# Products of constants in a two-layer trunk's gate and attention, w_glu multiplied whole, and GpSimd's preparation behind a marker

## The chip, the core and the metric

The kernel runs on one core of a Trainium2 chip. Its five engines work side by side, each through its own instructions in order: TensorE (PE, matrix products into PSUM; PEld is its loading of weights), VectorE (DVE), ScalarE (ACT), GpSimd (POOL) and SyncE (SP, which issues most transfers). The metric is the time of one execution in microseconds (us).

## The reference

Two layers over 528 rows (16 learned meta tokens and 512 tokens) of width 1024. Cut to what matters, with every array float32:

```python
for l in range(2):
    hn = rms_norm(h, norm_mix_g[l])
    c_q, c_kv, k_r, u = split(hn @ w_in[l])
    attn = mla_mixer(c_q, c_kv, k_r, ...)       # 4 heads, causal softmax of (q_nope.k_nope + q_rope.k_rope)
    y = complex diagonal state space over u     # 32 groups of 16 channels, 64 states, from a_re, a_im, log_dt, b, c, d
    g = gelu(y)
    ssm = g * sigmoid(g @ w_glu[l])             # w_glu is 512 x 512
    h = h + concat(rms_norm(attn), rms_norm(ssm)) @ w_o[l]
    hn = rms_norm(h, norm_ffn_g[l])
    h = h + (silu(hn @ w_gate[l]) * (hn @ w_up[l])) @ w_down[l]     # hidden width 2816
return rms_norm(h, final_norm_g)[:, 16:]
```

## The kernel before

Everything lies transposed in SBUF: 128 features on the partitions, the rows along the columns. The residual is eight tiles `h` of 128 x 528. The last layer's own part works on the 512 tokens alone.

**Products.** `product` (L268) multiplies one tile of weights with the normalised input. A weight tile comes in by DMA as `raw`. Either it is used whole (`FULL` lists the weights of each layer for which that holds): one float32 product for each 128 x 128 block, at L266. Or it is split: ScalarE casts it to `whi` (L254), VectorE or GpSimd subtracts to get the rest `wlo` (L198, the helper of all two-operand steps), the input is split into a high and a low part in the same way, and each block takes three products (high by high, weight's high by input's low, weight's low by input's high) at L278. With 528 columns each is done in two halves of 264. In layer 0 `w_glu` is whole, in layer 1 it is split, and so is its input `gs`.

**FFN.** `ffn` goes through 22 hidden tiles in three phases of 7, 7 and 8. For each hidden tile it does the gate product into `ga` and the up product into `ua` (eight blocks k = 0 to 7 each), then ScalarE and VectorE form `hid`; at the end of a phase eight down tiles `da` follow. The first gate product of a layer comes right behind the attention's output product: its inputs x[0] to x[7] are made one after the other by ScalarE (L311) and VectorE (L312) as the rows of `h` get their last addend. The sums of squares of the norm (`nacc`, L353) and their spreading over the partitions (`nrb`, L372) are pinned into the first up and the second gate product.

**Order.** The code gives no fixed list: generators are stepped in turn, a scheduler puts each engine's instructions in order by what is ready, and `after(...)` pins an instruction behind another one.

**Preparation of layer 1's state space.** While layer 0's FFN runs, `prep` makes layer 1's tables. `prep_small` computes the parameters on VectorE, by many steps on small tiles (`e`, `q`, `eh`, `el`: powers of the eigenvalues). Then come four quarters; each forms tables `tab` from `eh` and `el` (in layer 1's case on GpSimd, then copied by ScalarE at L595), and two sets of matrices: `bc` from `cc`, then `X`, `Xt`, `C`, `Ct` on GpSimd, transposes on TensorE, a tile `K` with `skip` added, and DMAs out to DRAM. A GpSimd step is placed as soon as its inputs are ready.

**Attention.** `scores` (L1064 to L1070) fills one PSUM block `sc` for each block of queries, the softmax follows on VectorE and ScalarE, `values` transposes the probabilities on TensorE into `ptr` (L1104), copies them to `PT` and multiplies with v into `pvo` (L1125). Between these stand the steps of the state-space scan: `va` (L744) and `ya` (L779 and L780; `S` is its carried state, made by GpSimd). At the program's start 14 products of zeros, bf16 and 512 columns wide, run before any data is there (L221).

Of the kernel before, what the change touches and what calls it, by code (L numbers as in the profile page):

```python
# [22 lines left out]
L = SEQ + NM  # L23
# [19 lines left out]
SING = 0  # L43
WHOLE = 1
PINF = (18, 6)
ACTSW = (0,0)
WIN = ([4,5,7,8,9,6,0,1,2,3],[4,5,0,1,2,3,7,8,9,6])
KB = 1
# [33 lines left out]
          gelu="V", amlo="P", split="V", wmix="P", small="V", ropem="V", nsq="VVVVVVVV", hs="V", woa="P", wos="P")  # L82
WC = 1024

FULL = (("in", "uq", "uk", "uv", "glu", "att", "pv"), ())
SW = 528
LOW, HIGH = 6, 6
BACK = 32
# [14 lines left out]
def trunk(ctx: ExitStack, tc: tile.TileContext, A, out, dbg=None):  # L103
# [151 lines left out]
        tt(lo_on, lo[:, :n], raw[:, :n], hi[:, :n].bitcast(F32), ALU.subtract)  # L255
        return hi, lo

    def product(acc, w, off, xs, cols=(0, L), pins={}, skew=False):
        c0, n = cols[0], cols[1] - cols[0]
        parts = 1 if n <= whole[0] else 2  # L260
        hw = n // parts
        n = len(xs)
        if len(w) == 1:
            for k in range(n):
                for a in range(parts):
                    T.matmul(acc[:, a, 0:hw], w[0][:, off + k * 128:off + (k + 1) * 128], xs[k][:, c0 + a * hw:c0 + (a + 1) * hw],  # L266
                             start=k == 0, stop=k == n - 1)
            return  # L268
        hi, lo = w
        terms = [(k, wt, xi) for k in range(n) for wt, xi in ((hi, 0), (hi, 1), (lo, 0))]  # L270
        if skew:

            terms = [(k, wt, xi) for j in range(n + 1) for k, wt, xi in ((j, hi, 0), (j, lo, 0), (j - 1, hi, 1)) if 0 <= k < n]
        for j, (k, wt, xi) in enumerate(terms):
            c = slice(off + k * 128, off + (k + 1) * 128)
            for a in range(parts):
                with after(pins.get(j)):
                    T.matmul(acc[:, a, 0:hw], wt[:, c], xs[k][:, xi, c0 + a * hw:c0 + (a + 1) * hw],  # L278
                             start=j == 0, stop=j == len(terms) - 1)
# [401 lines left out]

    def prep(l, ea, eb):
        yield from prep_small(l)
        for q in range(4):
            yield from prep_quarter(l, q, ea, eb)

    def prep_quarter(l, q, ea, eb):
        yield from prep_tables(l, q, ea, eb)
        for u in range(2):
            yield from prep_mats(l, q * 2 + u, ea, eb)  # L690
# [170 lines left out]
    def layer(l, nin, nout, nxt):  # L861
# [190 lines left out]
        def scores(hd, Ps):  # L1052
            Pw, off = wide("P"), 0
            for i in range(first_q, 5):
                n, w = (16 if i == 0 else 128), ends[i]
                acc = acc2("sc") if i == 4 else acc1("sc", SCB[i]).unsqueeze(1)
                spans = [(0, 0, max(256, w))] if i < 4 else [(0, 0, HALF), (1, HALF, HALF)]
                qs = slice(tt0[i], tt0[i] + 128)
                for a, s0, sn in spans:
                    o, ks = acc[:, a, 0:sn], slice(s0, s0 + sn)  # L1060
                    if "att" in FULL[l]:
                        T.matmul(o, qn[hd][:, qs], kn[hd][:, ks], start=True, stop=False)
                    for j, (qi, ki) in enumerate(((0, 0), (0, 1), (1, 0))) if "att" not in FULL[l] else ():
                        T.matmul(o, qn[hd][:, qi, qs], kn[hd][:, ki, ks], start=j == 0, stop=False)  # L1064
                    T.matmul(o, qr[hd // 2][:, hd % 2, qs], kr[:, 0, ks], start=False, stop=False)

                    T.matmul(o, qr[hd // 2][:, hd % 2, qs], kr[:, 1, ks], start=False, stop=i == 4 and a == 0)
                dg = acc[:, 0, 0:16] if i == 0 else acc[:, 0, w - 128:w] if i < 4 else acc[:, 1, 136:264]
                mw = 16 if i == 0 else 128
                T.matmul(dg, identb, maskb[:, 0:mw], start=False, stop=True)  # L1070
                sv = acc[0:n, 0, 0:w] if i < 4 else acc[0:n, :, 0:HALF]
                Pi = Pw[:, off:off + w]
                off += w
                po = Pi[0:n, 0:w] if i < 4 else halves(Pi)[0:n]
                st3 = np_.tile([128, 4], F32, tag="st", name="st")
                V.tensor_reduce(out=st3[0:n, 1:2], in_=sv, axis=AX.X if i < 4 else AX.XY, op=ALU.max, negate=True)

                f = rq[0:n, i - first_q:i - first_q + 1]
                mul(V, st3[0:n, 1:2], st3[0:n, 1:2], f)
                S.activation(po, sv, AF.Exp, bias=st3[0:n, 1:2], scale=f, accum_out=st3[0:n, 2:3])  # L1080
                V.reciprocal(out=st3[0:n, 3:4], in_=st3[0:n, 2:3])
                if on("pn", i) is S:
                    S.activation(Pi[0:n, 0:w], Pi[0:n, 0:w], AF.Copy, scale=st3[0:n, 3:4])
                else:
                    on("pn", i).tensor_scalar(out=Pi[0:n, 0:w], in0=Pi[0:n, 0:w], scalar1=st3[0:n, 3:4], scalar2=None, op0=ALU.mult)
                Ps[i] = Pi
                yield

        def values(hd, Ps):
# [6 lines left out]
            for j in range(5):  # L1096
                sn, s0 = (16 if j == 0 else 128), tt0[j]
                x = PT[j]
                b0 = base[j]
                pt = acc2("ptr").rearrange("p a b -> p (a b)") if j == 0 and not c0 else acc1("ptr", PTR[j])  # L1100
                for i in range(max(j, first_q), 5):
                    n = 16 if i == 0 else 128
                    c = 512 if i == 0 else (i - max(j, 1)) * 128
                    T.transpose(pt[0:sn, c:c + n], Ps[i][0:n, s0:s0 + sn], ident[0:n, 0:n])  # L1104
                w = (L if not c0 else 512) if j == 0 else 128 * (5 - j)
                if "pv" in FULL[l]:
                    if j % 2:
                        V.tensor_copy(x[0:sn, 0, b0:b0 + w].bitcast(F32), pt[0:sn, 0:w])
                    else:
                        S.copy(x[0:sn, 0, b0:b0 + w].bitcast(F32), pt[0:sn, 0:w])  # L1110
                else:
                    split((x[0:sn, 0, b0:b0 + w], x[0:sn, 1, b0:b0 + w]), pt[0:sn, 0:w])
                yield
# [160 lines left out]
        for ph in FFN_PHASES:  # L1274
            hid = []
            last = t0 + ph == NHT
            for i in range(t0, t0 + ph):
                wg = wload(A["w_gate"][l, i], V if i >= ONP[0] else P)
                ga = acc2("ga")
                product(ga, wg, 0, nf.xs, nat, {PINF[1]: nf.spread} if i == 1 else {})  # L1280
                if i == 0:
                    nf.F()
                wu = wload(A["w_up"][l, i], V if i >= ONP[1] else P)
                ua = acc2("ua")
                product(ua, wu, 0, nf.xs, nat, {PINF[0]: nf.summed} if i == 0 else {})
                nf.R()
                ev_up(i, ga, ua, hid)
                if i >= NXT[1]:

                    with after(latest(S) if i == NXT[1] else None):  # L1290
                        step(nxt, 2, NXT[0])
# [164 lines left out]
```

## Time and profile before

Three runs took 1321.73, 1325.82 and 1332.43 us. The execution that was profiled took 1328.52 us, with a span of 1326.0 us.

| What | Value |
|---|---|
| median of three runs | 1325.82 us |
| profiled execution, its span | 1328.52 us, 1326.0 us |
| TensorE's mean granted clock over the span | 0.977 |
| share of the span busy: PE, DVE, ACT, POOL | 96%, 59%, 32%, 25% |
| PE's share of the chain that ended last | 72% |
| lines with the largest share of that chain | da, ua and ga at L278: 18%, 18% and 17% |

Busy time counts instructions that run, not what they achieve: a product at half clock is busy for twice as long. The granted clock is a share of full speed, 1.00 being 2.4 GHz. A bracket behind a row of a timeline names the idle time ahead of the row and the instruction that ended it.

### The profile page before, as it was taken

How to read it: one execution, taken by the hardware profiler on the slowest of the kernel's cores; microseconds unless marked ns; L12 is line 12 of the kernel's file. 1: busy time of each engine (PE TensorE's matmuls, PEld its weight loads, DVE VectorE, ACT ScalarE, POOL GpSimd, SP SyncE). 2: the span in 40 equal slices, each digit the busy share in tenths (PEclk: the TensorE clock that was granted, in tenths of full speed). 3: DMA queues.
4: the chain of work that ended last, by engine and by line, in shares of the span. 5: the costliest groups of instructions: out<-in, count | busy, mean ns of one | idle time of the engine just before them, and what ended most of it. 6: DMA issues, size and time to landing. Idle time of an engine off the chain costs nothing.

```text
span 1326.0 us, 20502 instructions
## 1 busy us (share of the span) xinstructions
PE 1276.6 (96%) x8242; PEld 1149.1 (87%) x8242; DVE 779.5 (59%) x1467; ACT 427.5 (32%) x693; POOL 328.4 (25%) x311
## 2 busy tenths in 40 slices
PE   9989999989899999999999999999899999999996
PEld 7777887989899999999999999889788788788885
DVE  8875584496964555355554389665854445435545
ACT  4112454243232222132333226553422222222231
POOL 3101233730572333024204355157200000000001
PEclk9989999999989999999999999699999999999998
DMA  6576442222234344334335447022232323233321
GB/s 219 150 193 160 146 138 88 80 80 82 65 119 147 105 118 107 103 104 120 104 104 161 126 129 216 25 64 65 80 96 86 106 95 91 84 110 92 91 88 64
DMA packets 82575, 145.92 MB, mean 110 GB/s; under 512 B 23344, under 2 KB 49456, under 8 KB 82480
## 3 DMA queue, kind: packets, MB, share of 16 engines
q1 hardware_dynamic: 81184, 143.42, 36.7%
q8 instruction: 64, 1.05, 0.3%
q10 hardware_dynamic: 1296, 1.20, 0.3%
q14 instruction: 31, 0.25, 0.1%
HBM read 121.17 MB, written 23.43 MB: 109 GB/s over the span
## 4 chain that ended last, share of the span: by engine, by line
PE 72%; DVE 9%; ACT 2%; POOL 2%; issue 1%; DMA 1%; DVEq 0%; SPq 0%; POOLq 0%; ACTq 0%
PE da L278 18%; PE ua L278 18%; PE ga L278 17%; PE acc L278 10%; DVE h L198 1%; DVE sq L198 1%; PE acc L266 1%; PE nrb L372 1%; PE pvo L1125 1%; PE pvo L1122 1%; PE nacc L353 1%; DVE wo L198 1%; DVE wlo L198 1%; PE pk L660 1%; POOL tab L198 1%
## 5 line engine op out<-in xcount | busy, mean ns | idle before, releaser
L254 ACT CAST whi<-raw 128x1024 fp32r<-128x1024 f32 (+3 forms) x174 | 174.0, 1000 | 552.5 <-issue 172.3
L278 PE MATMUL ga<-x,whi 128*128 128x264 f32 (+1 forms) x1056 | 227.5, 323 | 6.8 <-ACT x L311 4.7
L278 PE MATMUL da<-hid,whi 128*128 128x264 f32 (+2 forms) x1088 | 227.0, 317 | 2.0 <-ACT hid L308 1.4
L278 PE MATMUL ua<-x,whi 128*128 128x264 f32 (+1 forms) x1056 | 226.3, 323 | 0.0
L278 PEld LDWEIGHTS ga<-x,whi 128*128 128x128 f32 x1056 | 164.4, 189 | 24.8 <-ACT x L311 4.5
L278 PEld LDWEIGHTS da<-hid,whi 128*128 128x128 f32 x1088 | 168.4, 189 | 16.2 <-ACT hid L308 1.6
L198 DVE TENSOR_TENSOR wlo<-raw,whi 128x1024 fp32r<-128x1024 f32 (+1 forms) x130 | 165.7, 1274 | 23.5 <-ACT whi L254 21.4
L278 PEld LDWEIGHTS ua<-x,whi 128*128 128x128 f32 x1056 | 165.5, 191 | 15.6
L278 PE MATMUL ua<-x,wlo 128*128 128x264 f32 (+1 forms) x528 | 142.6, 324 | 4.5 <-DVE wlo L198 4.5
L278 PE MATMUL da<-hid,wlo 128*128 128x264 f32 (+2 forms) x544 | 144.6, 319 | 0.9 <-DVE wlo L198 0.6
L278 PE MATMUL ga<-x,wlo 128*128 128x264 f32 (+1 forms) x528 | 142.1, 323 | 0.2 <-POOL wlo L198 0.2
L198 POOL TENSOR_TENSOR wlo<-raw,whi 128x1024 fp32r<-128x1024 f32 (+2 forms) x44 | 96.8, 2200 | 138.5 <-ACT whi L254 138.5
L198 DVE TENSOR_TENSOR h<-da,h 128x528 f32<-128x528 f32 (+2 forms) x50 | 33.9, 677 | 130.6 <-PE da L278 130.5
L278 PEld LDWEIGHTS ua<-x,wlo 128*128 128x128 f32 x528 | 88.7, 190 | 12.5 <-DVE wlo L198 4.7
L278 PEld LDWEIGHTS da<-hid,wlo 128*128 128x128 f32 x544 | 91.1, 190 | 9.4 <-DVE wlo L198 2.2
L198 POOL TENSOR_TENSOR o<-h,nr 128x256 f32<-128x256 f32 x8 | 6.1, 798 | 364.3 <-ACT nr L376 364.3
L278 PEld LDWEIGHTS ga<-x,wlo 128*128 128x128 f32 x528 | 88.1, 189 | 8.4 <-POOL wlo L198 0.7
L198 DVE TENSOR_TENSOR g<-ua,R 128x528 f32<-128x528 f32 (+1 forms) x44 | 30.8, 699 | 108.4 <-PE ua L278 108.2
L198 DVE TENSOR_TENSOR g<-ga,nr 128x528 f32<-128x528 f32 (+1 forms) x44 | 30.8, 699 | 84.9 <-PE ga L278 84.0
L266 PE MATMUL acc<-x,raw 128*128 128x264 f32 x320 | 76.9, 396 | 0.3 <-ACT x L706 0.3
L266 PEld LDWEIGHTS acc<-x,raw 128*128 128x128 f32 x320 | 61.3, 195 | 11.6 <-ACT x L706 0.7
L278 PE MATMUL acc<-x,whi 128*128 128x264 f32 (+1 forms) x320 | 53.2, 285 | 0.0
(280 smaller groups left out, 2087.8 us busy)
## 6 DMA issues: line engine op xcount, KB each, us to landing
raw<-w_gate SPq DMA_DIRECT2D x44, 512.0 KB, 3.6
raw<-w_up SPq DMA_DIRECT2D x44, 512.0 KB, 3.6
raw<-w_down SPq DMA_DIRECT2D x32, 448.0 KB, 3.4
raw<-w_in SPq DMA_DIRECT2D x20, 512.0 KB, 4.0
mat<-mat SPq DMA_DIRECT2D x16, 528.0 KB, 4.0
mt<-k SPq DMA_DIRECT2D x16, 512.0 KB, 5.1
raw<-w_down SPq DMA_DIRECT2D x16, 512.0 KB, 3.6
mat<-tab SPq DMA_DIRECT2D x16, 272.0 KB, 2.6
```

The lines of the kernel that those rows point to most:

```text
L198: e.tensor_tensor(out=o, in0=a, in1=b, op=op)
L254: S.copy(hi[:, :n], raw[:, :n])
L266: T.matmul(acc[:, a, 0:hw], w[0][:, off + k * 128:off + (k + 1) * 128], xs[k][:, c0 + a * hw:c0 + (a + 1) * hw], start=k == 0, stop=k == n ...
L278: T.matmul(acc[:, a, 0:hw], wt[:, c], xs[k][:, xi, c0 + a * hw:c0 + (a + 1) * hw], start=j == 0, stop=j == len(terms) - 1)
L353: T.matmul(acc[:, i:i + 1], x[:, a:a + 128], ones[:, 0:1], start=x is sqs[0], stop=x is sq)
L372: T.matmul(p[:, a - c0:b - c0], y[0:b - a, j:j + 1].to_broadcast([b - a, 128]), ident[0:b - a, 0:b - a], start=True, stop=True)
L660: T.matmul(pk[0:16, g * 128:(g + 1) * 128], bb1[:, g, :], C[:, g * 144 + 16:g * 144 + 144], start=True, stop=True)
L1122: T.matmul(acc[:, a, 0:w], vs[hd // 2, j][0:sn, hd % 2 * 128:hd % 2 * 128 + 128], PT[j][0:sn, 0, c:c + w].bitcast(F32), start=j == 0, stop ...
L1125: T.matmul(acc[:, a, 0:w], vs[hd // 2, j][0:sn, vi, hd % 2 * 128:hd % 2 * 128 + 128], PT[j][0:sn, pi, c:c + w], start=j == 0 and z == 0, s ...
```

## The change

It has four parts.

1. A new helper `fill(to, n)` issues n products of a constant bf16 tile (`identb`) by itself, 512 columns wide, each pinned behind the TensorE instruction before it. Nobody reads what it writes; the next true product into that bank starts it anew.
2. At a layer's first gate tile the product stops behind block k = 6; then come `FILL[l]` such products into `ua`'s bank, 12 in layer 0 and 6 in layer 1; then block k = 7, pinned behind them. The up product comes only after that.
3. In layer 1's attention, heads 2 and 3 get two of them ahead of each block of scores (four blocks a head) and one ahead of each group of transposes (five a head): 26 in all. And `w_glu` of layer 1 is multiplied whole.
4. In `prep`, GpSimd first copies one column of the last-made parameter tile (`begun`), and each step of the first quarter is pinned behind that copy.

```diff
+FILL = (12, 6)
...
-FULL = (("in", "uq", "uk", "uv", "glu", "att", "pv"), ())
+FULL = (("in", "uq", "uk", "uv", "glu", "att", "pv"), ("glu",))
...
+    def fill(to, n):
+
+        for _ in range(n):
+            with after(latest(T)):
+                T.matmul(to, identb, identb.unsqueeze(1).to_broadcast([128, 4, 128]), start=True, stop=True)
+
-    def product(acc, w, off, xs, cols=(0, L), pins={}, skew=False):
+    def product(acc, w, off, xs, cols=(0, L), pins={}, skew=False, ks=None):
...
+            if ks is not None and k not in ks:
+                continue
...
     def prep(l, ea, eb):
         yield from prep_small(l)
+
+        P.tensor_copy(small("begun")[:, 0:1], prm["hi"][1][:, HIGH - 1, 0:1])
+        begun = latest(P)
         for q in range(4):
-            yield from prep_quarter(l, q, ea, eb)
+            g = prep_quarter(l, q, ea, eb)
+            while True:
+                with after(begun if q == 0 else None):
+                    if next(g, g) is g:
+                        break
+                yield
...
                 acc = acc2("sc") if i == 4 else acc1("sc", SCB[i]).unsqueeze(1)
+                if l == 1 and hd >= 2:
+                    fill(acc[:, 0, 0:512], 2)
...
+                if l == 1 and hd >= 2:
+                    fill(pt[:, 0:512], 1)
...
-                product(ga, wg, 0, nf.xs, nat, {PINF[1]: nf.spread} if i == 1 else {})
-                if i == 0:
+                if i:
+                    product(ga, wg, 0, nf.xs, nat, {PINF[1]: nf.spread} if i == 1 else {})
+                    ua = acc2("ua")
+                else:
+
+                    product(ga, wg, 0, nf.xs, nat, ks=range(7))
+                    ua = acc2("ua")
+                    fill(ua[:, 0, 0:512], FILL[l])
+                    with after(latest(T)):
+                        product(ga, wg, 0, nf.xs, nat, ks=(7,))
                     nf.F()
                 wu = wload(A["w_up"][l, i], V if i >= ONP[1] else P)
-                ua = acc2("ua")
```

On TensorE, in layer 0's first gate tile (`ga` and `ua` are the gate and up accumulators, `x` the normalised input), from block k = 6 on, before:

```order
L278 MATMUL ga<-x,whi 128x264 x2
L278 MATMUL ua<-x,whi 128x264 x4
L278 MATMUL ga<-x,whi 128x264 x2
L278 MATMUL ga<-x,wlo 128x264 x2
L278 MATMUL ga<-x,whi 128x264 x2
L278 MATMUL ua<-x,wlo 128x264 x2
L278 MATMUL ua<-x,whi 128x264 x4
L278 MATMUL ga<-x,whi 128x264 x2
L278 MATMUL ga<-x,wlo 128x264 x2
L278 MATMUL ua<-x,wlo 128x264
L353 MATMUL nacc<-cst,sq 128x1 x5
```

and in the changed kernel (the first of the twelve pairs in the middle stands for all):

```order
L287 MATMUL ga<-x,whi 128x264 x4
L287 MATMUL ga<-x,wlo 128x264 x2
L263 LDWEIGHTS identb
L263 MATMUL ua<-identb 128x512
...
L287 MATMUL ga<-x,whi 128x264 x4
L287 MATMUL ga<-x,wlo 128x264 x2
L362 MATMUL nacc<-cst,sq 128x1 x5
L287 MATMUL ua<-x,whi 128x264 x4
```

The eleven products into `ua` that were mixed in ahead of `nacc` have moved behind it, and twelve products of constants stand between blocks 6 and 7, behind block 6's six products.

On GpSimd, at the start of the preparation for layer 1, before:

```order
L198 TENSOR_TENSOR bc<-bc,cc 128x128 x6
L198 TENSOR_TENSOR bc<-bc 128x128 x2
L198 TENSOR_TENSOR bc<-bc,cc 128x128 x2
L198 TENSOR_TENSOR bc<-bc 128x128
L198 TENSOR_TENSOR X<-bc,pf 128x512
L198 TENSOR_TENSOR bc<-bc 128x128
L198 TENSOR_TENSOR Xt<-bc,pf 128x512
L198 TENSOR_TENSOR C<-bc,pw 128x576
L198 TENSOR_TENSOR Ct<-bc,pw 128x576
```

and in the changed kernel:

```order
L199 TENSOR_TENSOR bc<-bc,cc 128x128 x3
L199 TENSOR_TENSOR bc<-bc 128x128
L199 TENSOR_TENSOR bc<-bc,cc 128x128
L199 TENSOR_TENSOR bc<-bc 128x128
L694 COPY begun<-eh 128x1
L199 TENSOR_TENSOR tab<-eh,el 128x8x36
L199 TENSOR_TENSOR tabt<-eh,el 128x288
L199 TENSOR_TENSOR tab<-eh,el 128x8x36
L199 TENSOR_TENSOR tabt<-eh,el 128x288
L199 TENSOR_TENSOR bc<-bc,cc 128x128 x3
L673 MEMSET K_4319 16x4x128
L199 TENSOR_TENSOR skip<-cst,skips 16x64 x2
```

Six steps of `bc` stay ahead of the copy `begun`; all else, the `X` and `C` steps among it, is now behind it, and the first tables come right after it.

On TensorE, at head 2's last block of scores in layer 1's attention, before:

```order
L1065 MATMUL sc<-kr,q 128x264
L1067 MATMUL sc<-kr,q 128x264
L1064 MATMUL sc<-k,q 128x264 x3
L1065 MATMUL sc<-kr,q 128x264
L1067 MATMUL sc<-kr,q 128x264
L1070 LDWEIGHTS identb
L1070 MATMUL sc<-maskb,identb 128x128
L779 MATMUL ya<-U,mt 128x64
L780 MATMUL ya<-S,mt 128x64
```

and in the changed kernel:

```order
L263 LDWEIGHTS identb
L263 MATMUL sc<-identb 128x512
L1083 MATMUL sc<-k,q 128x264 x3
L1084 MATMUL sc<-kr,q 128x264
L1086 MATMUL sc<-kr,q 128x264
L1083 MATMUL sc<-k,q 128x264 x3
L1084 MATMUL sc<-kr,q 128x264
L1086 MATMUL sc<-kr,q 128x264
L1089 LDWEIGHTS identb
L1089 MATMUL sc<-maskb,identb 128x128
L796 MATMUL ya<-U,mt 128x64
L797 MATMUL ya<-S,mt 128x64
```

All eight products of constants of head 2's scores now stand ahead of the `ya` that needs the state `S`; none stands between that `ya` and head 1's transposes behind it.

## Rows read from the trace of the kernel before

**Rows 1.** Page, part 1: busy us, share of span, count of instructions.

```profile
PE 1276.6 (96%) x8242; PEld 1149.1 (87%) x8242; DVE 779.5 (59%) x1467; ACT 427.5 (32%) x693; POOL 328.4 (25%) x311
```

**Rows 2.** Windows: length, busy us of PE PEld DVE ACT POOL, clock, DMA.

```profile
284.00:301.00 17.00, 12.56 (x78) 11.87 (x76) 13.29 (x16) 7.08 (x10) 3.37 (x2) 0.80 0.21 61
352.00:369.00 17.00, 12.50 (x90) 12.29 (x90) 16.93 (x31) 3.39 (x5) 14.85 (x16) 0.90 0.25 72
386.00:398.00 12.00, 9.37 (x61) 8.73 (x60) 4.66 (x5) 4.47 (x8) 12.00 (x12) 0.86 0.35 112
834.00:858.00 24.00, 21.29 (x91) 17.89 (x90) 11.78 (x31) 12.20 (x30) 2.40 (x5) 0.57 0.07 17
881.00:890.50 9.50, 7.54 (x49) 6.91 (x48) 4.71 (x16) 3.92 (x8) 4.00 (x3) 0.82 0.01 3
```

**Rows 3.** Timeline, PE, layer 0's first gate: start, duration, work, [idle before].

```profile
293.67 0.81 PE L278 MATMUL ga<-x,whi 128*128 128x264 f32 x2 [3.61 <-ACT x L311]
294.28 1.08 PE L278 MATMUL ua<-x,whi 128*128 128x264 f32 x4
...
299.25 1.56 PE L353 MATMUL nacc<-cst,sq 128*128 128x1 f32 x10
```

**Rows 4.** Waits of PE, 350 to 400 us: total, times, longest.

```profile
PE ua L278 <- DVE wlo L198: 4.5, 1, 4.5
```

**Rows 5.** Waits of PE in layer 1's attention, 820 to 892 us.

```profile
PE ya L780 <- POOL S L198: 1.8, 1, 1.8
PE nacc L353 <- POOL g L198: 1.0, 1, 1.0
```

**Rows 6.** Chain of waits, 780 to 965 us: start, length, what.

```profile
858.83 2.85 PE acc L278 x24
...
958.89 5.57 PE ua L278 x24
```

**Rows 7.** Timeline of PE, products of constants at the start of the program.

```profile
1.35 5.72 PE L221 MATMUL idle<-idle 128*128 128x512 bf16 x14 [1.35 <-POOL idle L218]
```

**Rows 8.** Timeline of PE, layer 0's w_glu, multiplied whole.

```profile
225.59 5.61 PE L266 MATMUL acc<-u,raw 128*128 128x264 f32 x24 [1.08 <-ACT gl L1153]
```

**Rows 9.** Timeline of DVE at layer 0's first gate, block 6's low part.

```profile
294.53 0.76 DVE L312 SCALAR_TENSOR_TENSOR x<-h,gains,x 128x528 fp32r<-128x528 f32 x1
```

**Rows 10.** Groups of DVE by form, 352 to 366 us: busy us, mean ns.

```profile
L198 DVE TENSOR_TENSOR el<-el,tq 128x32 f32<-128x32 f32 x2 | 2.4, 1214 | 0.0
```

**Rows 11.** Timeline of POOL, its preparation for layer 1.

```profile
347.31 5.28 POOL L198 TENSOR_TENSOR bc<-bc,cc 128x128 f32<-128x128 f32 x6 [44.94 <-DVE cc L198]
...
356.02 1.11 POOL L198 TENSOR_TENSOR Xt<-bc,pf 128x512 f32<-128x512 f32 x1
...
363.22 2.07 POOL L198 TENSOR_TENSOR Xt<-bc,pf 128x512 f32<-128x512 f32 x1
365.37 1.63 POOL L198 TENSOR_TENSOR X<-X,Xt 128x512 f32<-128x512 f32 x1
373.17 2.30 POOL L198 TENSOR_TENSOR tab<-eh,el 128x288 f32<-128x288 f32 x2 [6.17 <-DVE eh L198]
...
404.10 1.58 POOL L198 TENSOR_TENSOR tab<-tab,tabt 128x288 f32<-128x288 f32 x2
```

**Rows 12.** Groups of DVE by form, 366 to 373.2 us.

```profile
L198 DVE TENSOR_TENSOR eh<-eh,tq 128x32 f32<-128x32 f32 x4 | 0.6, 186 | 0.0
```

**Rows 13.** Timeline of PE, layer 0's first down tile.

```profile
383.38 0.73 PE L278 MATMUL da<-hid,whi 128*128 128x264 f32 x4
```

**Rows 14.** Timeline of ACT, casts of two later down tiles.

```profile
409.72 0.94 ACT L254 CAST whi<-raw 128x896 fp32r<-128x896 f32 x1 [2.75 <-PE da L278]
414.83 0.94 ACT L254 CAST whi<-raw 128x896 fp32r<-128x896 f32 x1 [4.16 <-PE da L278]
```

**Rows 15.** Timeline of PE at layer 1's first gate.

```profile
943.55 0.50 PE L278 MATMUL ga<-x,whi 128*128 128x512 f32 x1 [2.19 <-DVE x L312]
...
953.58 1.13 PE L372 MATMUL nrb<-cst,nw 128*128 128x128 f32 x8 [0.70 <-DVE nw L337]
```

## The prediction, made before the result was known

> **What bounds the kernel now.** The page's first part comes first: TensorE is busy for 1276.6 of 1326.0 us [rows 1]. So time can be gained in three ways only: fewer products, fewer waits of TensorE, or fewer stretches in which it runs at half clock. Next come the windows around the places that the change touches [rows 2]; there the reader is to see the granted clock beside PE's busy time. A mean clock of 0.80 over 17 us means that 40% of it, 6.8 us, ran at 1.2 GHz and not 2.4, since half clock for a share s gives 1 - s/2. In the same way 3.4 us of 352 to 369, 3.4 us of 386 to 398, 20.6 us of 834 to 858 and 3.4 us of 881 to 890.5 ran at half clock. Last come timelines and waits, for what stands ahead of each fall. The fall at the gate follows a wait of 3.61 us [rows 3], the one in layer 0's FFN a wait of 4.5 us [rows 4], the one in attention a wait of 1.8 us for the scan's state [rows 5].
>
> **Prices.** A split product of 256 columns costs 2.85 / 24 = 0.119 us [rows 6]; a pass of 512 columns at full clock 5.57 / 24 = 0.232 us [rows 6]. The bf16 products at the program's start, the same form as the new ones, cost 5.72 / 14 = 0.41 us each [rows 7], which I take as the price at half clock. A whole float32 product of 264 columns costs 5.61 / 24 = 0.234 us [rows 8], so 0.227 us for 256.
>
> **The gate of layer 0: +3.4 us.** The wait of 3.61 us is for x[6] [rows 3], and the order puts the twelve products behind block 6, so they do not cover it; the clock falls as before. Block 6's last input is made at 294.53 + 0.76 = 295.3 [rows 9]. Four more products at half clock (1.08 / 4 less overlap, 0.22 us each, [rows 3]) put the first new product at about 296.2. The half-clock time of 6.8 us that began inside the wait lasted to about 299.9, since the norm's products at 299.25 [rows 3] are the last slow ones. So nine new products run at 0.41 and three at 0.23: 4.4 us. Then block 7's six products (0.7 at full clock), and the eleven up products that used to stand here come later (11 x 0.12 = 1.3). Before, the path from 296.2 to the norm's products at 299.25 took 3.05. The sum is 4.4 + 0.7 + 1.3 - 3.05 = +3.4. If all twelve ran at full clock it would be 2.8 + 2.0 - 3.05 = +1.7; if the clock stayed low throughout, 4.9 + 1.3 + 2.4 - 3.05 = +5.6. I take the middle, since nothing in the order shortens the wait that lowers the clock.
>
> **GpSimd behind the marker: -7 us.** In 352 to 369 VectorE is busy for 16.93 of 17 us and GpSimd for 14.85 [rows 2], and VectorE's 128 x 32 steps take 1.21 us [rows 10]. In 366 to 373.2, where GpSimd soon stands idle for 6.17 us [rows 11], steps of the same size take 0.19 us [rows 12]. After the change GpSimd waits at the marker while VectorE makes its parameters, so each such step gives back about 1.0 us. Four of them ahead of the `wlo` for which TensorE waits 4.5 us [rows 4] are enough to end that wait. With it goes its half-clock time, worth 3.4 / 2 = 1.7. That is 6.2. If eight such steps get faster, the marker comes at about 373 - 8 = 365.
>
> Against it stands GpSimd's work behind the marker. It is 14.4 us of `bc`, `X` and `C` steps (352.6 to 367.0, [rows 11]) and 32.5 us of tables and the rest (373.17 to 405.68, [rows 11]), about 46, so it ends near 411. Today's ends at 405.7. The tables matter because ScalarE copies them in front of the casts of the down tiles, in order. The second stretch, 386 to 398, shows what that costs now: PE idle 12 - 9.37 = 2.63 us plus 1.7 for half clock, 4.3 in all [rows 2]. After the change the first down product comes 6.2 earlier than 383.38 [rows 13], at about 377, and a tile takes 414.83 - 409.72 = 5.1 us [rows 14]; the eighth cast is due at 377 + 7 x 5.1 = 413. 411 is just in time, the third tile's cast a little late. So I let this second place gain 0.8 only. Both stalls wholly gone would be -10.5; the first gain partly eaten by later casts, -4.
>
> **Attention of layer 1: -11 us.** In 834 to 858 PE's busy time of 21.29 us holds 20.6 us at half clock [rows 2]; at full clock it is 21.29 - 10.3 = 11.0. The sixteen new products in and ahead of this stretch cost 16 x 0.232 = 3.7. Head 2's eight stand ahead of the `ya` that waits 1.8 us for the state [rows 5]; 8 x 0.232 = 1.86, so they fill that wait, and the clock has no reason to fall there. ScalarE's 12.20 and VectorE's 11.78 us of work [rows 2] then come to bear, so I leave 1.8 us of waits: 11.0 + 3.7 + 1.8 = 16.5 for 24, -7.5. `w_glu`: 96 split products become 32 whole ones, 32 x 0.227 - 96 x 0.119 = -4.1, and ten new products among the transposes cost 2.3: -1.8. The split of `gs`, four casts and four subtractions, also goes; I count it as zero, because it lies beside TensorE's products. In 881 to 890.5, a wait of 1.0 us for `g` [rows 5] lowers the clock, worth 1.7; PE idles 1.96 there in all [rows 2]; half of it is saved by what comes earlier: -1.7. If every wait goes, -15; the other end is the second rival, below.
>
> The Trainium skill's page "FP8 and Floating Point Precision", section "TensorE Precision Notes", says that true FP32 takes four passes through the array. By that `w_glu` would cost 32 x 4 x 0.119 = 15.2 and the sum would be 7.9 us worse; the trace disagrees, with 0.234 us for 264 columns, two passes.
>
> **The gate of layer 1: +1.1 us.** TensorE waits 2.19 us for x[6] too [rows 15], at full clock. Six new products cost 6 x 0.232 = 1.4, and two up products (0.46) that ran ahead of the wait now come behind it; the later wait of 0.70 for the norm [rows 15] goes. The ends are 0 and +1.9.
>
> **The sum.** 3.4 - 7.0 - 11.0 + 1.1 = -13.5 us, against the profiled execution's 1328.5: 1315. That execution lies 2.7 above the median of 1325.8, on which the forecast stands: **1312 us**. Its own range, from the ends, is 1302 to 1322.
>
> **Rivals.** About 1%, 13 us, is what a measurement of this kernel can tell from no change; the three runs lie 10.7 apart.
>
> *The clock falls in attention all the same* (0.16). No new product stands between the `ya` and head 1's transposes. At full clock these chains wait for softmax and copies sooner, and a new fall there would meet sixteen products at 0.41. For it: ScalarE and VectorE have as much work there as PE. Against it: the fall now comes at the one long wait, which is filled. C would be 16 x 0.41 + 2.3 - 4.1 - 1.8 = +3.0 in place of -11, the total +0.5: 1326.
>
> *GpSimd's block of work comes late* (0.14), the rival that ends slower. With VectorE busy, an `Xt` took 2.07 us in place of 1.11 [rows 11]. If the 46 us behind the marker stretch by a factor f, they end at 365 + 46f, and the eighth cast, due at 413, is late by that difference; each late us costs 1.65 (2.63 idle brought 4.3). B is -10.5 + 1.65 x late. The total is zero at B = +6.5, late 10.3, f = 1.27. At f = 1.35 it is +6: 1332. Beyond f = 1.43 it is slower by over 1%, which takes 0.08 of the 0.14. Against it: the stretch after 373, with the same kind of work, already holds VectorE's steps at their usual length.
>
> *All new products lie in waits* (0.11). Every term at its lower end: 1.7 - 10.5 - 15 + 0 = -23.8, 1302.
>
> *Whole products take four passes* (0.02). All else as forecast, w_glu costs 15.2 in place of 7.3: 1320. The row of layer 0's w_glu speaks against it.
>
> **How the numbers follow.** The forecast has 0.57; its range reaches across the 1% line at 1312.5, so I give 0.33 of it to faster and 0.24 to the same. With 0.11 from the lower rival, faster has 0.44; with 0.16, 0.02 and 0.06 the same has 0.48; slower has 0.08. The range, 1302 to 1330, leaves out the tail below the lowest case and the upper part of the late GpSimd, some 0.05 and 0.1.
>
> **What would show it.** Right: a granted clock near 1.00 from 834 to 858, no wait of 1.8 for the state; no 4.5 us wait for `wlo` near 364 and VectorE's small steps at 0.2 us there; the last tables at about 411 and no down tile waiting more than some 2 us for its cast; w_glu's products 0.227 us apart; new products at 0.41 in layer 0's gate and 0.23 in layer 1's, with the 3.61 us wait still ahead of block 6. Wrong: a clock below 0.8 in attention, ScalarE's casts of the later down tiles waiting for `tab`, or new products at the gate that do replace the wait.

## The result and the profile after

The changed kernel took 1334.78 us (median of 19 runs, 1331.46 to 1339.32) against 1326.29 for the kernel before on the same chip: ratio 1.0058, 95% interval 1.0041 to 1.0075, so 5 to 10 us slower where 13.5 less had been forecast. Its profiled execution took 1337.82 us, with a span of 1335.9. TensorE's busy time rose by 6.3 us against [rows 1]:

```profile
PE 1282.9 (96%) x8254; PEld 1149.1 (86%) x8254; DVE 778.6 (58%) x1463; ACT 424.2 (32%) x687; POOL 319.1 (24%) x310
```

The windows of the changed kernel at the places of [rows 2], moved by as much as the same work stands later there, with the first gate of layer 1 as a sixth (columns as in [rows 2]):

```profile
289.30:306.30 17.00, 11.65 (x63) 8.29 (x62) 13.11 (x15) 6.03 (x9) 2.37 (x1) 0.80 0.18 62
357.30:374.30 17.00, 17.00 (x142) 17.00 (x142) 14.73 (x56) 6.58 (x10) 5.17 (x8) 1.00 0.29 86
387.70:399.70 12.00, 4.28 (x28) 4.07 (x28) 11.90 (x4) 0.00 (x0) 12.00 (x12) 0.75 0.08 10
842.20:866.20 24.00, 22.28 (x140) 19.19 (x139) 13.78 (x40) 13.55 (x35) 5.09 (x7) 0.86 0.08 23
889.20:898.70 9.50, 8.65 (x67) 7.52 (x66) 5.95 (x18) 4.09 (x7) 5.43 (x4) 1.00 0.09 17
942.90:966.90 24.00, 20.69 (x85) 14.99 (x84) 16.19 (x26) 8.52 (x13) 4.86 (x2) 0.86 0.20 60
```

The second row is the forecast come true: clock 1.00 and no idle time where there had been 0.90 and a wait of 4.5 us. In the third TensorE is busy for 4.28 of 12 us (9.37 before), while VectorE and GpSimd are busy all the time. The fourth and fifth have most of their clock back, as forecast, but TensorE is as busy in the fourth as before: it now holds products of constants and, at its end, the first of w_glu's, which came behind this window before. The sixth, at 1.00 before, is at 0.86.

For the sum by stages, the time between landmarks of TensorE's timeline in every kernel of this study, in us: the front (to layer 0's first gate product), layer 0's gate with the first seven hidden tiles, the first eight down tiles, the rest of layer 0, layer 1 up to its first gate product, its gate with its first seven hidden tiles, and from there to the last down product. Behind them the ratio to the kernel before in the timed runs.

| Kernel | front | gate 0 | down 1 | rest 0 | attention 1 | gate 1 | rest 1 | ratio (95%) |
|---|---|---|---|---|---|---|---|---|
| before | 285.4 | 97.9 | 47.0 | 272.1 | 233.4 | 84.2 | 291.2 | 1 |
| the change | 290.7 | 94.4 | 52.8 | 272.7 | 232.3 | 87.6 | 290.7 | 1.0058 (1.0041 to 1.0075) |
| marker alone | 287.4 | 89.9 | 55.0 | 272.7 | 229.5 | 86.5 | 291.2 | 1.0034 (1.0007 to 1.0062) |
| w_glu whole alone | 293.8 | 97.7 | 46.3 | 272.1 | 231.8 | 86.2 | 290.7 | 1.0038 (1.0010 to 1.0065) |
| gates alone | 285.8 | 101.1 | 47.0 | 272.1 | 229.5 | 84.5 | 291.2 | 1.0031 (1.0011 to 1.0052) |
| attention's 26 alone | 293.1 | 97.8 | 46.3 | 272.1 | 228.9 | 86.0 | 289.8 | 0.9995 (0.9967 to 1.0024) |
| marker with a pause | 292.5 | 90.1 | 54.6 | 272.7 | 226.6 | 84.2 | 291.3 | 1.0009 (0.9980 to 1.0037) |
| gates, ahead of block 6 | 285.2 | 101.1 | 45.8 | 272.1 | 230.7 | 83.5 | 291.3 | 0.9989 (0.9960 to 1.0018) |
| attention, 8 only | 285.1 | 101.6 | 46.6 | 272.1 | 227.4 | 86.5 | 291.3 | 0.9980 (0.9954 to 1.0005) |
| those three together | 285.1 | 93.4 | 54.4 | 272.7 | 227.0 | 82.1 | 291.3 | 0.9983 (0.9953 to 1.0012) |
| marker, paced | 292.1 | 90.1 | 41.0 | 273.3 | 229.3 | 86.5 | 291.3 | 0.9937 (0.9913 to 0.9962) |
| paced, with 8 and gate 1 | 285.6 | 91.1 | 41.0 | 273.3 | 227.1 | 83.5 | 291.6 | 0.9862 (0.9821 to 0.9902) |
| the change, no marker | 285.4 | 100.9 | 46.9 | 272.1 | 231.7 | 87.7 | 290.7 | 1.0051 (1.0019 to 1.0084) |
| the change, w_glu split | 284.1 | 95.0 | 53.0 | 272.7 | 231.6 | 86.3 | 289.8 | 1.0019 (0.9992 to 1.0046) |

First comes how much one profile of a stage scatters. TensorE's order in the front is the same in all fourteen, and it took 284.1 to 293.8 us. Six kernels have the old order in attention 1 (before, marker alone, gates alone, marker with a pause, gates ahead of block 6, marker paced): 226.6 to 233.4. So only what repeats in the kernels that share a part is taken for its effect; and the 5.3 us by which the change's profile is behind in the front are scatter.

### The profile page after: what moved, and what is told of

Its sections match the earlier page's. It is cut to its first block, busy times and chain, and to the rows that moved or that the text cites. A ratio compares the mean times of both kernels' runs of the same rounds, so it can differ in the third digit from the quotient of the medians.

```text
span 1335.9 us, 20503 instructions
## 1 busy us (share of the span) xinstructions
PE 1282.9 (96%) x8254; PEld 1149.1 (86%) x8254; DVE 778.6 (58%) x1463; ACT 424.2 (32%) x687; POOL 319.1 (24%) x310
## 4 chain that ended last, share of the span: by engine, by line
PE 76%; DVE 13%; DMA 5%; ACT 2%; issue 2%; POOL 1%; SPq 1%; DVEq 0%; ACTq 0%; POOLq 0%
PE da L287 18%; PE ua L287 18%; PE ga L287 18%; PE acc L287 9%; PE acc L273 2%; DMA ud<-u 1%; DVE sq L199 1%; DVE h L199 1%; PE pvo L1143 1%; DMA yd<-ys 1%; PE nrb L381 1%; PE pvo L1146 1%; DMA mat<-tab 1%; DVE wlo L199 1%; PE pk L669 1%
## 5 line engine op out<-in xcount | busy, mean ns | idle before, releaser
L199 DVE TENSOR_TENSOR wlo<-raw,whi 128x1024 fp32r<-128x1024 f32 (+1 forms) x130 | 170.3, 1310 | 17.5 <-ACT whi L255 15.2
L199 POOL TENSOR_TENSOR wlo<-raw,whi 128x1024 fp32r<-128x1024 f32 (+2 forms) x42 | 90.6, 2156 | 147.7 <-ACT whi L255 141.6
L287 PEld LDWEIGHTS ua<-x,wlo 128*128 128x128 f32 x528 | 87.7, 188 | 7.8
```

Of the source, the lines that this page charges most:

```text
L199: e.tensor_tensor(out=o, in0=a, in1=b, op=op)
```

## Where the time went

**The down tiles.** The waits of TensorE in the changed kernel from 350 to 410 us:

```profile
PE da L287 <- DVE wlo L199: 7.7, 1, 7.7
```

The 4.5 us wait for a `wlo` of [rows 4] is gone, and one of 7.7 us for another `wlo` has come. VectorE's timeline there:

```profile
383.25 8.76 DVE L1285 SCALAR_TENSOR_TENSOR g<-g 128x528 f32<-128x528 f32 x1
...
392.74 5.05 DVE L199 TENSOR_TENSOR wlo<-raw,whi 128x896 fp32r<-128x896 f32 x1
```

The step g <- (th + 1) * g lasted 8.76 us; in VectorE's timeline of the kernel before the same step lasted 0.69:

```profile
382.87 0.69 DVE L1264 SCALAR_TENSOR_TENSOR g<-g 128x528 f32<-128x528 f32 x1
```

GpSimd's timeline beside the long one:

```profile
371.78 0.18 POOL L694 COPY begun<-eh 128x1 f32<-128x1 f32 x1 [11.59 <-DVE eh L199]
...
391.31 1.46 POOL L199 TENSOR_TENSOR tab<-eh,el 128x288 f32<-128x288 f32 x1
...
399.58 1.36 POOL L199 TENSOR_TENSOR tabt<-eh,el 128x288 f32<-128x288 f32 x1
406.08 1.23 POOL L199 TENSOR_TENSOR C<-bc,pw 128x576 f32<-128x576 f32 x1 [5.14 <-PE pt L657]
```

GpSimd waited for the marker (11.59 us), and then ran from 371.8 to 400.9 without a gap. VectorE's held step ended at 392.0, inside a step of GpSimd that lasted 1.46 us instead of 0.9; the `wlo` behind it was held for 5.05. So here VectorE got in in the middle of the run, after nine of GpSimd's steps and again after five.

A run without a gap is not enough for this. In the kernel before GpSimd was busy for all of 386 to 398 [rows 2], and indeed from 383.9 to 405.7, and VectorE's longest step beside it was this:

```profile
397.76 1.92 DVE L198 TENSOR_TENSOR wlo<-raw,whi 128x896 fp32r<-128x896 f32 x1 [1.95 <-ACT whi L254]
```

**w_glu.** TensorE's group for it in the changed kernel, from 860 to 885 us (busy us, mean ns), and one piece of its timeline:

```profile
L273 PE MATMUL acc<-u,raw 128*128 128x256 f32 x64 | 14.6, 379 | 0.0
```

```profile
866.59 4.48 PE L273 MATMUL acc<-u,raw 128*128 128x256 f32 x20
```

32 products of the program stand as 64 rows, 4.48 / 20 = 0.224 us each: 14.3 us, against 96 x 0.119 = 11.4 for the split ones. The row of [rows 8] was of the same kind: its 24 rows were 12 products.

**The gates.** TensorE's timeline at layer 0's first gate tile, and at layer 1's:

```profile
298.94 0.81 PE L287 MATMUL ga<-x,whi 128*128 128x264 f32 x2 [3.61 <-ACT x L320]
300.61 0.81 PE L287 MATMUL ga<-x,whi 128*128 128x264 f32 x2 [0.86 <-DVE x L321]
...
301.66 4.40 PE L263 MATMUL ua<-identb 128*128 128x512 bf16 x12
305.71 0.84 PE L287 MATMUL ga<-x,whi 128*128 128x264 f32 x4
```

```profile
950.20 0.79 PE L287 MATMUL ga<-x,whi 128*128 128x512 f32 x1 [2.87 <-ACT x L320]
...
952.45 2.78 PE L263 MATMUL ua<-identb 128*128 128x512 bf16 x6
```

The wait of 3.61 us ahead of block 6 is as it was, and twelve products of constants behind it cost 4.40 us. At layer 1's gate the wait is 2.87 where it was 2.19 [rows 15]; the two up products that ran ahead of it no longer do. The clock fell behind it in this profile, and the six products cost 2.78 us, 0.46 each.

## The experiments

**Marker alone.** The edit against the kernel before:

```diff
     def prep(l, ea, eb):
         yield from prep_small(l)
+        P.tensor_copy(small("begun")[:, 0:1], prm["hi"][1][:, HIGH - 1, 0:1])
+        begun = latest(P)
...
+                with after(begun if q == 0 else None):
```

> The kernel before with the marker in GpSimd's preparation and nothing else. Theory 1 (read from the two traces): the 4.5 us wait for wlo goes, worth 6 to 7 us with its half-clock time, but GpSimd's steps then come without a gap while the first down tiles are made, a VectorE step of FFN work is held up for over 4 us there, and TensorE waits about 8 us for the second down tile's wlo; net within 2 us of before. Theory 2 (the prediction): -7 us, VectorE's steps at the down tiles at their usual 0.7 to 1.8 us. On the front of the program, up to layer 0's first gate product, both kernels have the same order of work on TensorE; the profile of the changed one reached it at 290.7 and that of before at 285.5. If that is scatter between executions, this kernel's profile may lie anywhere near those two; if a part of the change caused it, a kernel with that part alone shows 290.7 and the others 285.5.

Measured: ratio 1.0034 (1.0007 to 1.0062). By stages, gate 0 fell from 97.9 to 89.9 and down 1 rose from 46 or 47 to 55.0. The rows are VectorE's held step, then GpSimd's last step of the run and the first behind it:

```profile
375.50 16.37 DVE L1281 SCALAR_TENSOR_TENSOR g<-g 128x528 f32<-128x528 f32 x1
```

```profile
390.41 0.89 POOL L199 TENSOR_TENSOR tabt<-eh,el 128x288 f32<-128x288 f32 x1
400.54 1.22 POOL L199 TENSOR_TENSOR C<-bc,pw 128x576 f32<-128x576 f32 x1 [9.24 <-PE pt L657]
```

The step lasted 16.37 us and ended at 391.87, 0.6 us after the last step of GpSimd's run (390.41 + 0.89). The next step of VectorE, `g` from a PSUM bank, took its usual 0.71. Theory 1 holds for the mechanism; by stages the net is +1, by the timed runs +1 to +8 us.

**w_glu whole alone.**

```diff
-FULL = ((..., "pv"), ())
+FULL = ((..., "pv"), ("glu",))
```

> The kernel before with layer 1's w_glu multiplied whole and nothing else. Theory 1: each whole product of 256 columns stands as two rows of 0.224 us in the trace, so 32 of them cost 14.3 us against 11.4 for the 96 split ones: +2.9 us, less whatever the missing casts and subtractions give back, so +1 to +3. Theory 2 (the prediction): 0.227 us for each, -4.1 us.

Measured: ratio 1.0038 (1.0010 to 1.0065), 1 to 9 us slower, and attention 1 at 231.8 where the middle of the six profiles with the old order is 229.5. The forecast's -4.1 is outside the interval; +2.9 is inside it.

**The gates alone.** The edit is the gate's part of the change.

> The kernel before with the products of constants at the two first gate tiles (12 and 6) and nothing else. Theory 1: the wait ahead of block 6 stays, +3.2 us in layer 0; in layer 1 the wait grows to 3.3 us because the up products no longer stand in it, the clock falls to half for some 7 us, and that gate costs +3.4; together about +6.5. Theory 2 (the prediction): +3.4 and +1.1, clock in layer 1's gate at 1.00, together +4.5.

Measured: ratio 1.0031 (1.0011 to 1.0052), 1.5 to 7 us slower. Gate 0 is 3.2 us longer (101.1 against 97.9), as both theories had it. In gate 1 the clock stayed at 1.00 in this profile, and the stage took 84.5; with the same order it took 86.3, 87.6 and 87.7 in three other kernels. Theory 1's +3.4 for layer 1 does not repeat, and neither does +1.1.

**Attention's 26 products alone.**

```diff
+                if l == 1 and hd >= 2:
+                    fill(acc[:, 0, 0:512], 2)
...
+                if l == 1 and hd >= 2:
+                    fill(pt[:, 0:512], 1)
```

> The kernel before with the 26 products of constants in layer 1's attention and nothing else, w_glu split. Theory 1: from the end of layer 0's last down tile to layer 1's first gate product -4 us: the half-clock stretch shrinks from about 20 us to about 7, and the products themselves cost 6. Theory 2 (the prediction): -7.5 in the stretch of half clock, -1.7 at the norm, +2.3 for ten products: -7.

Measured: ratio 0.9995 (0.9967 to 1.0024): nothing. The window of 58 us from 120 us behind layer 0's end (columns as above), first before, then gates alone (old order there too), then this kernel:

```profile
822.40:880.40 58.00, 55.29 (x361) 49.93 (x359) 41.64 (x82) 33.41 (x71) 21.34 (x21) 0.82 0.21 66
```

```profile
825.90:883.90 58.00, 52.81 (x374) 48.01 (x372) 42.83 (x84) 35.82 (x77) 22.73 (x22) 0.91 0.23 70
```

```profile
829.30:887.30 58.00, 54.91 (x407) 49.07 (x406) 42.92 (x93) 34.18 (x74) 23.91 (x23) 0.98 0.22 68
```

Clock 0.82 is 20.9 us at half speed, 0.91 is 10.4, 0.98 is 2.3. The profile of before, from which the term was worked out, shows twice the half-clock time of most others: five of the six profiles with the old order have 10.4 or less. From 10.4 there are (10.4 - 2.3) / 2 = 4.0 us to gain in clock, and 54.91 - 52.81 = 2.1 of idle time was filled; the products cost 26 x 0.232 = 6.0. That leaves nothing. In the change and its two variants, which have the same 26 products, this window is at 0.94, so 7.0 us at half speed, and the stage took 231.6 to 232.3: the gain in clock is smaller there.

**A pause in GpSimd's run.**

```diff
             V.scalar_tensor_tensor(out=g, in0=th, scalar=1.0, in1=g, op0=ALU.add, op1=ALU.mult)
+            if l == 0 and i in (5, 6):
+                P.tensor_copy(small("begun")[:, 1:2], g[:, 0:1])
```

> The kernel with the marker alone, and one thing more: in layer 0, behind VectorE's step g <- (th + 1) * g of hidden tiles 5 and 6, GpSimd copies one column of its result, so GpSimd's run of steps has to pause until that VectorE step is done. Theory P (GpSimd's steps without a gap keep the VectorE step out; in the kernel with the marker alone it lasted 16.4 us and ended when GpSimd's run ended): the step shrinks to some 3 us (until GpSimd reaches the copy) and then ends, the wait of 11.4 us for the second down tile's wlo goes, and the kernel gains 6 to 8 us on before: about 1319. Rival Q (the step is long for another reason, say its own inputs or the down phase): it stays above 8 us and the time stays at about 1330.

Measured: ratio 1.0009 (0.9980 to 1.0037), down 1 still at 54.6. VectorE's timeline, then GpSimd's:

```profile
380.70 2.86 DVE L1281 SCALAR_TENSOR_TENSOR g<-g 128x528 f32<-128x528 f32 x1
383.66 0.71 DVE L199 TENSOR_TENSOR g<-ua,R 128x528 f32<-128x528 f32 x1
384.29 13.74 DVE L199 TENSOR_TENSOR wlo<-raw,whi 128x896 fp32r<-128x896 f32 x1
```

```profile
383.83 0.17 POOL L1283 COPY begun<-g 128x1 f32<-128x1 f32 x1
...
396.18 0.89 POOL L199 TENSOR_TENSOR tabt<-eh,el 128x288 f32<-128x288 f32 x1
```

The step was let in at the pause (380.70 + 2.86 = 383.6), and then the next one that reads two tiles of SBUF, `wlo`, was held for 13.74 us, to 398.0; GpSimd's run ended at 397.1. The expected gain did not come, but the pause shows the cause: GpSimd's run holds VectorE's step, first one step with two SBUF inputs and then the next, and where GpSimd waits, VectorE gets in. (In the changed kernel it also got in without such a stop.) Between them `g` from PSUM took 0.71.

**Products ahead of block 6.**

```diff
-                    product(ga, wg, 0, nf.xs, nat, ks=range(7))
+                    product(ga, wg, 0, nf.xs, nat, ks=range(6))
                     ua = acc2("ua")
-                    fill(ua[:, 0, 0:512], FILL[l])
+                    fill(ua[:, 0, 0:512], EARLY[l])                  # (14, 9)
                     with after(latest(T)):
-                        product(ga, wg, 0, nf.xs, nat, ks=(7,))
+                        product(ga, wg, 0, nf.xs, nat, ks=(6, 7))
```

> The kernel before with 14 and 9 products of constants at the two first gate tiles, ahead of block 6, so inside the wait, and not behind it. Theory (the place decides: a product behind the wait costs its own time and leaves the clock to fall): granted clock stays at 1.00 at both gates, layer 0's gate costs 1 us less than before and not 3.1 more, layer 1's 0 to 2 us less; together -1 to -3 us against before, and 4 to 6 less than with the products behind block 6. Rival: the clock falls all the same, since block 6's low part and block 7 still come late; then +2 to +4.

Measured: ratio 0.9989 (0.9960 to 1.0018). The windows of the two gates:

```profile
285.20:302.20 17.00, 14.85 (x85) 12.48 (x86) 14.27 (x23) 6.40 (x10) 4.73 (x2) 0.84 0.17 48
934.90:958.90 24.00, 22.82 (x107) 17.47 (x106) 19.70 (x31) 10.90 (x16) 4.87 (x2) 1.00 0.26 80
```

In layer 0 the rival is right: 14 products fill the wait down to 0.60, but waits of 1.21 and 0.30 for blocks 6 and 7 follow, the clock falls to 0.84, and the stage is at 101.1. In layer 1 the theory is right: clock 1.00, and 83.5 us, below all seven profiles with the old gate 1 (84.2 to 86.5); the two other kernels with these nine products took 82.1 and 83.5.

**Eight products in attention.**

```diff
+                if l == 1 and hd == 2:
+                    fill(acc[:, 0, 0:512], 2)
```

> The kernel before with eight products of constants only, two ahead of each block of head 2's scores in layer 1: as much work (1.9 us) as the wait for the scan's state is long. Theory (26 products gave back the clock and cost as much as that): the wait of 1.73 us goes, the half-clock stretch behind it (10 us in most profiles of the old order) goes or shrinks, -3 to -5 us in the stage from layer 0's end to layer 1's gate, where kernels with the old order took 229.5 us or more. Rival: the later short waits of the transposes lower the clock anyway, within 1 us of before.

Measured: ratio 0.9980 (0.9954 to 1.0005). Attention 1 took 227.4 us, and 227.0 and 227.1 in the two other kernels that have it, against 229.5 in the middle of the old order: -2 to -2.5, though one profile of the old order has 226.6. The wait for the state is gone.

**The three together.**

> The three of this set together: marker with the pause, products ahead of block 6, eight products in attention, w_glu split. If the theories above hold the sum is about -7 - 2 - 4 = -13 us against before: 1313. If only the marker's holds, about -6: 1320.

Measured: ratio 0.9983 (0.9953 to 1.0012). The sum did not come, because the pause did not help (down 1 at 54.4).

**GpSimd paced.** Behind the marker only the first quarter's tables follow at once. All else is pinned behind a copy of one column of the newest hidden tile, a new copy for every hidden tile from the ninth on; five of these tiles take three pieces and not two.

```diff
...
+                if q == 0 and k == 2:
+                    for _ in range(DELAY):                           # 5
+                        yield
+                if (q or k >= 2) and prm["hid"] is not seen:
+                    seen = prm["hid"]
+                    P.tensor_copy(small("begun")[:, n % 16:n % 16 + 1], seen[:, 0, NM:NM + 1].bitcast(F32))
+                    begun, n = latest(P), n + 1
-                with after(begun if q == 0 else None):
+                with after(begun):
...
```

> The kernel with the marker alone, but with GpSimd's work behind it broken up: only the first quarter's tables follow the marker at once, and all the rest of the preparation is pinned, piece by piece, behind copies of one column of the newest hidden tile, from hidden tile 8 on, so that no run of GpSimd's steps is longer than some 10 us. Theory P (a VectorE step that meets GpSimd's run waits for the run's end; a pause alone only hands the wait to the next VectorE step, as the wlo of 13.7 us did): no VectorE step in layer 0's FFN over 5 us, the 4.5 us wait near 365 and the waits of 8 to 11 us at the first down tiles both gone, the stretch from layer 0's first gate product to the end of its first eight down tiles 8 to 12 us shorter than before's 144.9, the kernel at about 1316 to 1319. Rival: the tables alone, some 9 us of steps, do the same harm at the same place; then 1326 or more.

Measured: ratio 0.9937 (0.9913 to 0.9962), 1319.41 us. From layer 0's first gate product to the end of the first down tiles, before and then paced:

```profile
285.40:430.40 145.00, 134.21 (x1040) 132.31 (x1041) 98.91 (x222) 41.39 (x60) 54.91 (x51) 0.95 0.33 99
```

```profile
292.10:423.30 131.20, 127.35 (x1030) 126.68 (x1031) 86.28 (x221) 38.76 (x53) 11.95 (x9) 0.99 0.30 91
```

131 us and not 145; TensorE's idle time fell from 10.8 to 3.9, of which 3.61 is the gate's, and the clock rose from 0.95 to 0.99. GpSimd's timeline behind the marker is now this:

```profile
368.93 0.18 POOL L695 COPY begun<-eh 128x1 f32<-128x1 f32 x1 [60.44 <-DVE eh L200]
369.07 0.93 POOL L200 TENSOR_TENSOR tab<-eh,el 128x288 f32<-128x288 f32 x1
...
373.11 3.02 POOL L200 TENSOR_TENSOR tab<-tab,tabt 128x288 f32<-128x288 f32 x2
448.83 0.45 POOL L707 COPY begun<-hid 128x1 f32<-128x1 f32 x1 [72.70 <-ACT hid L318]
```

After 7 us of tables GpSimd stands idle for 72.70 us. VectorE's longest step in layer 0's FFN behind the marker took 3.42 us. Both old waits are gone, and so are the waits for casts behind `tab` in the down tiles. So what Theory P forecast came, and its rival did not. But the edit does two things: it moves GpSimd's work out of the first down tiles and breaks it up, and the gain in this stretch can come from the first alone; no run here parts the two. Later, GpSimd still ran for up to 23.7 us with no gap above 0.1 us (651.2 to 674.9) beside VectorE, and the rest of layer 0 took 1.3 us longer than before. In the timed runs the gain is 5 to 11.5 us, less than the 13.8 of this stretch in one profile.

**Paced, with eight products in attention and nine ahead of block 6 in layer 1.**

> The same with eight products of constants ahead of head 2's scores and nine ahead of block 6 of layer 1's first gate tile; nothing at layer 0's gate, w_glu split. If the parts add up: -8 for GpSimd's pacing, -2.5 for the scores (measured as a ratio of 0.998), -2 for layer 1's gate: about 1313 to 1315. If pacing fails, about 1322.

Measured: 1310.11 us (six runs), ratio 0.9862 (0.9821 to 0.9902): faster than before by 13 to 24 us, and by the medians than the changed kernel by about 25. Its windows of attention and of gate 1:

```profile
811.10:869.10 58.00, 54.33 (x403) 48.95 (x402) 47.05 (x96) 35.51 (x77) 24.18 (x23) 0.98 0.22 69
918.10:942.10 24.00, 22.78 (x107) 17.44 (x106) 19.67 (x31) 10.86 (x16) 4.86 (x2) 1.00 0.25 78
```

**The change without its marker.**

> The changed kernel without the marker, all else as in the change. If the parts measured alone add up (marker 1.0034), it is 4 us faster than the changed kernel: about 1330. By the prediction's price of the marker it would be 7 us slower: 1342.

Measured: ratio 1.0051 (1.0019 to 1.0084), the same as the change's 1.0058. So in the change the marker gains and loses about as much; neither the 4 us nor the prediction's 7 are seen.

**The change with w_glu split.**

> The changed kernel with w_glu of layer 1 split as before, all else as in the change. If a whole product costs 0.45 us (two rows of 0.224) it is 3 us faster than the changed kernel, with the measured ratio of w_glu alone (1.0038) up to 5: about 1330 to 1332. By the prediction's price it would be 4 us slower: 1339.

Measured: ratio 1.0019 (0.9992 to 1.0046), about 5 us faster than the change, where +2.9 by the products had been worked out; the two intervals just meet, so 1 us or 9 would fit too. The attention stage of the profiles does not show it (231.6 against 231.7 and 232.3 with w_glu whole); layer 1 as a whole is 2 to 3 us shorter. The prediction's price had the other sign.

## Why the prediction was wrong, step by step

**GpSimd behind the marker: -7 forecast, about +1 by stages.** Its first half was right and too small: gate 0 lost 7.8 us, not 6.2. The step that failed is "I let this second place gain 0.8 only". It asked when GpSimd's tables come, and let ScalarE's casts wait for them. What came instead is VectorE kept out: one step of 0.7 us lasted 8.8 to 16.4 us while GpSimd ran without a gap, TensorE waited 7.7 to 11.4 us for the `wlo` behind it, and down 1 rose by 6 to 9 us. The slower rival had the place and, as GpSimd's 29 us without a gap show, the wrong engine: GpSimd's steps there took 1.1 us for an `Xt`, not 2.07, and VectorE paid. The prediction read two engines' contention off [rows 10, 11], where each slowed the other a little, and took these sizes as the bounds; the argument "VectorE's steps at their usual length" after 373 was nearly right for the old order (up to 1.92 us) and did not carry over to the new one.

The Trainium skill's page "SBUF — State Buffer", section "Who interferes with whom", says that a VectorE instruction with two SBUF inputs and a GpSimd instruction that reads SBUF exclude each other, and that the second to issue waits until the first finishes. By that a step of 0.7 us would wait for one step of GpSimd, 1 to 2 us by an estimate from [rows 11]. The traces agree on who excludes whom (steps with an input from PSUM kept their 0.71 us), and the kernel before agrees on how long (1.92 us at most in its first down tiles). With the marker alone it differs: the step was held through some seventeen steps in a row, 16.37 us, and the measurement decides.

**Attention: -11 forecast, +2.5 in its stage.** Two terms failed. "32 x 0.227 - 96 x 0.119 = -4.1" took each row of the trace for a product. The order of the program shows 32 products and the trace 64 rows of 0.224, so it is +2.9 and not -4.1. That was the rival to which 0.02 was given. The Trainium skill's page "FP8 and Floating Point Precision", section "TensorE Precision Notes", gives four passes for true FP32, 15.2 us here by an estimate at 0.119 a pass; the trace agrees, with 14.3, and the prediction's sentence that it disagrees was the misreading. The other term is the base: "20.6 us at half clock" was one execution's, and 10.4 is the commoner figure, which takes 5 of the 7.5 us away. The eight products in the wait did what was said of them: the wait is gone, and the stage took 227.0 to 227.4 where they stand alone. With the eighteen others, 18 x 0.232 = 4.2 us of work, it took 228.9 and 231.6 with w_glu split.

**The gate of layer 0: +3.4 forecast, +3.2 measured.** Right by its own steps: the wait stays, and twelve products take 4.40 us behind it, at 0.37 each on the way from one clock to the other. With the marker it is +4 to +5 (94.4 and 95.0 against 89.9 to 90.1); one profile of the old order has 101.6 too, in the kernel with eight products in attention, with 13.5 us at half speed behind the wait.

**The gate of layer 1: +1.1 forecast, about +1 measured.** The prediction let the wait of 2.19 us stand at full clock and priced the six products at 1.4. In the kernel with the gates alone it came so (a wait of 2.17, the products 1.47 us); in the change's profile the wait was 2.87, the clock fell behind it, and they cost 2.78. Four kernels with it took 84.5, 86.3, 87.6 and 87.7, seven without it 84.2 to 86.5: about +1 in the middle, but the size is not settled. The clock of 1.00 in the profile of before was no rule there: five of the seven profiles of the old gate have 3.4 us at half speed.

**The sum.** With +3.2, +1, +2.5 and +1 the parts give about +8; the runs gave 5 to 10. The range ended at 1330. The measured time is 0.6% above before, inside the 1% that the prediction called the same, to which it gave 0.48; that this came true is luck, for 0.40 of it stood for the forecast's own sum and for a clock that stays low in attention, and neither is what the runs showed.

What stays open: why VectorE could get in between GpSimd's steps in the old order (1.2 us a step from 352 to 366, 1.92 at most from 383.9 to 405.7) and not, or only after many of them, in the new; no run here tells it. Nor is it settled why the marker alone is +4.5 by medians and +1 by stages.

## What to carry to other kernels

When GpSimd's work is moved so that it runs without a gap, look at which steps of VectorE with two SBUF inputs it meets, and let the range reach to a wait of the whole run, not of one instruction. Tying GpSimd's pieces to the work beside which they may run, and so away from the first down tiles, took the loss away here. Count a row's products against the program's order before dividing by them. Take a gain in clock from several profiles of the same order, and put products of constants inside a wait, for behind it they only cost their time; by the stages of the profiles they helped inside it in layer 1's gate and attention, and not in layer 0's gate, where two more waits follow.

## What the runs showed of the hardware beyond that

VectorE's steps that read two SBUF tiles were held for 8.76, 13.74 and 16.37 us by GpSimd's run, and for 1.92 at most by another run as gapless; steps with an input in PSUM beside the same runs took 0.71. TensorE's half-clock time is not fixed by the order of a stage's products: the same order in layer 1's attention had 20.9, 10.4 (four times) and 3.5 us of it, and the same front took 284.1 to 293.8 us.
